# Output projection of a hybrid encoder block in pairs of row blocks: half of its row tiles by seven products of sums instead of eight plain products

## The chip, the cores and the metric

The kernel runs on one core of a Trainium2 chip. The metric is device time in microseconds for one launch; a lower time is better. Before the change the median of three runs is 943.16 us (942.99 to 943.22). One further execution was recorded by the hardware profiler; it took 943.95 us.

The core has a matrix engine (TensorE, called PE in the profile, with its weight loads as PEld), a vector engine (VectorE, DVE), a scalar engine (ScalarE, ACT), a general engine (GpSimd, POOL), and SyncE (SP), which here issues the DMA transfers. Every engine has an instruction stream of its own and waits on semaphores for the others.

## The reference, cut to what matters

One layer: a normalisation, one input projection, windowed attention and a convolution group, both gated, and one output projection with a residual. Only the last lines are touched by the change:

```python
att = windowed_gqa(q, k, v, sink).reshape(B, L, W_ATT) * jax.nn.silu(g_att)
cnv = conformer_conv(c_val, c_glu, conv_w, conv_b, ln_w, ln_b) * jax.nn.silu(g_conv)
mixed = jnp.concatenate([att, cnv], axis=-1)
return z + jnp.einsum('ble,ed->bld', mixed, w_out)
```

`mixed` has 1024 columns: 512 of attention and 512 of the convolution. `w_out` is 1024 x 1024. There are 2304 rows (a prompt of 256 and a sample of 2048), 18 blocks of 128.

## The kernel before, in words

**Numbers in two parts.** Each float32 operand of a large product is split into a high part (`hi`, float32r, a rounding copy on ScalarE) and a low part (`lo`, the rest, a subtraction on VectorE). A product then takes three matmuls: hi x hi, hi x lo, lo x hi (`PASSES`, line 151).

**Two stages.** The first (up to about 605 us) is the input projection in 11 units of weights and two chunks of rows (`ORDER`, line 1068; `items`, line 1070), with the depthwise convolution (31 taps, line 946) on VectorE beside it and the LayerNorm of the convolution's result (`ln_block`, line 211) after it. The second is attention and the output projection, in time slots: `slot_step(s_, slot)` (line 625) has eight slots for each of NB + 2 steps. In step s_ the scores of block s_ are taken (`scores`, one per slot), and in the slots of the next step its probabilities are turned (`bank`, line 491), split and multiplied with v (`pv`, line 522) and merged (`merge`, line 543). Slots are counted through both stages here: slot t is step t // 8, place t % 8. The first 14 slots (`EARLY`) run among the last projection units, through `spread` (line 658); `mixing_open` (line 280), called at the ninth block of the last but one unit, first empties the queue of LayerNorm blocks and then opens the tiles for the mixing, whose places in memory the convolution and LayerNorm held; `attention_rest` (line 679) runs the others.

**The output projection.** The 1024 rows of `w_out` are eight row tiles e of 128; e = 0 to 3 belong to attention and 4 to 7 to the convolution. For block b, column half nh and row tile e, `outproj` (line 601) issues the three matmuls of 512 columns into a PSUM bank of that block and half; the bank gathers all eight e. After the last e, VectorE adds it to the rows of the input (`yo`, loaded by `load_x`), and a DMA stores them. From slot 14 on, every slot takes two such (nh, e) pieces, six matmuls. The last block's second half goes in two quarters of 256 columns, so that the end is short.

**Left operands.** `mix_conv` (line 578) multiplies the convolution's block by its gate on POOL, then splits it into parts: into `mch`, `mcl` for even blocks and into part of `rest` for odd ones. `merge` adds the two halves of the attention's result (VectorE), multiplies by the gate (POOL) and splits into `rest`. `rest` takes the place of the last projection weights and can be written only when the last projection is done.

**The right operand.** `presplit_wo(e)` (line 331) splits the row tiles of `w_out` in the first stage, at places listed in `split_at` (line 1190), and writes the parts to DRAM (`wod`). At the end of the first stage `load_wo` brings all 16 pieces of 512 KB into the tiles that the projection's operands leave (`xh`, `xl`), in the order e = 4 to 7, 0, 1, 2, 3; they stay there.

**What sets the order.** A planner orders the instructions of SP, ACT and DVE (in the first stage also PE's) by the times that it expects; under `manual_schedule` POOL, and from `attention_rest` on PE too, work in the order of the program. Python runs the program's order with a clock of ticks: `tick(ns)` ends each slot or projection group, `later(k, f)` puts f at the k-th tick from now. The taps of the convolution are let out by a credit: a tick gives ns, a tap costs 1.04 x 1167 + 135 ns (line 964), and `owe(ns)` takes credit away, so that other VectorE work puts taps off.

## Time and profile before

| | before |
|---|---|
| median of three runs | 943.16 us |
| the profiled execution | 943.95 us, span 941.9 us |
| PE busy | 935.6 us, 5794 matmuls |
| DVE busy | 744.4 us |
| ACT busy | 421.8 us |
| POOL busy | 293.3 us |
| output projection | 888 matmuls at line 609 |

The span runs from the first to the last instruction of the profiled execution. A row of the page's groups gives line, engine, operation, output<-inputs, shape and count, then busy us and mean ns of one, then the idle time of the engine just ahead of them with what ended it. A row of a timeline gives start, duration, engine, line, operation; "x6" are six merged instructions, and a bracket is idle time before it with its releaser. The matmuls of one group overlap at their ends, so the mean of one is longer than the distance between two; the chain of waits, which counts each stretch of time once, gives the distance.

### The profile page before, as it was taken

The numbers are of one execution on the slowest core, as the hardware profiler recorded it, in microseconds if no ns is written. First come the engines' busy times: TensorE is split into PE (matmuls) and PEld (weight loads), VectorE is DVE, ScalarE is ACT, GpSimd is POOL, SyncE is SP. The second block draws the span as 40 slices with busy tenths as digits, with TensorE's granted clock in tenths as the row PEclk, the third lists the DMA queues.
The fourth block names the chain that finished last, engine by engine and source line by source line (L and its number), as shares of the span: only waits on it lengthen the run. The fifth ranks groups of instructions, "written<-read, shape, count | busy, mean of one in ns | idle before, by whom it ended". The sixth has DMA issues, their size and how long they took to land.

```text
span 941.9 us, 16665 instructions
## 1 busy us (share of the span) xinstructions
PE 935.6 (99%) x5794; PEld 886.3 (94%) x5794; DVE 744.4 (79%) x1263; ACT 421.8 (45%) x1160; POOL 293.3 (31%) x490
## 2 busy tenths in 40 slices
PE   9999999999999999999999999999999999999998
PEld 8999999999999999999999999988888888888887
DVE  5579999997977879999996655677777677767773
ACT  7432022253457751011111356666666666656661
POOL 4320000173558400000000553755433242333332
PEclk9999999999999999999999999999999999999999
DMA  8575345676656595233333697975666556655512
GB/s 306 170 253 217 134 176 176 217 269 251 182 185 189 182 312 182 90 113 134 140 128 123 159 327 225 395 240 159 200 188 172 151 165 196 188 159 148 163 62 68
DMA packets 146211, 176.49 MB, mean 187 GB/s; under 512 B 40816, under 2 KB 108736, under 8 KB 146000
## 3 DMA queue, kind: packets, MB, share of 16 engines
q1 hardware_dynamic: 146128, 175.43, 57.8%
q8 instruction: 46, 0.75, 0.3%
q14 instruction: 37, 0.30, 0.1%
HBM read 112.69 MB, written 62.70 MB: 186 GB/s over the span
## 4 chain that ended last, share of the span: by engine, by line
PE 94%; DMA 2%; DVE 1%; SPq 1%; issue 0%; ACT 0%; POOL 0%; DVEq 0%; ACTq 0%; POOLq 0%
PE pj L863 43%; PE y L609 21%; PE pj L879 13%; PE O L533 5%; PE S L383 4%; PE pT_c L499 2%; PE pT_m L499 2%; PE pT_x L499 1%; DMA cd<-zn 1%; DMA bias<-in_bias_c 1%; PE qT L383 1%; PE lnu L240 0%; DMA xn<-in_z 0%; PE lnt L221 0%; DVE xt L772 0%
## 5 line engine op out<-in xcount | busy, mean ns | idle before, releaser
L863 PE MATMUL pj<-xh,ws 128*128 128x384 f32 (+1 forms) x1536 | 395.9, 338 | 0.1
L946 DVE SCALAR_TENSOR_TENSOR y<-us,cw,y 128x1167 f32<-128x1167 f32 x240 | 329.0, 1427 | 0.4
L863 PEld LDWEIGHTS pj<-xh,ws 128*128 128x128 f32 x1536 | 280.0, 188 | 0.4 <-ACT xh L1111 0.4
L863 PE MATMUL pj<-xl,ws 128*128 128x384 f32 (+1 forms) x768 | 260.9, 340 | 0.1
L609 PE MATMUL y<-wo,rest 128*128 128x512 f32 (+1 forms) x672 | 172.7, 394 | 0.0
L879 PE MATMUL pj<-ws,xh 128*128 128x256 f32 (+1 forms) x880 | 164.2, 284 | 0.3 <-DVE kn L1037 0.3
L863 PEld LDWEIGHTS pj<-xl,ws 128*128 128x128 f32 x768 | 144.1, 188 | 0.5 <-DVE xl L801 0.4
L609 PEld LDWEIGHTS y<-wo,rest 128*128 128x128 f32 x672 | 117.5, 189 | 21.4 <-DVE rest L566 0.3
L879 PEld LDWEIGHTS pj<-ws,xh 128*128 128x128 f32 (+1 forms) x880 | 136.1, 187 | 1.1 <-issue 0.4
L879 PE MATMUL pj<-ws,xl 128*128 128x256 f32 (+1 forms) x440 | 124.3, 283 | 0.0
L441 DVE CUSTOM_DVE_ANT_0 sb<-S,bias,vec 128x304 f32<-128x304 f32 (+5 forms) x144 | 74.5, 517 | 33.8 <-PE S L383 31.5
L453 ACT ACTIVATE sb<-sb,nm 128x304 f32<-128x304 f32 (+5 forms) x144 | 77.8, 540 | 48.9 <-DVE nm L441 48.2
L971 ACT ACTIVATE go<-pj 128x384 f32<-128x384 f32 x48 | 23.5, 489 | 149.8 <-PE pj L863 142.3
L879 PEld LDWEIGHTS pj<-ws,xl 128*128 128x128 f32 (+1 forms) x440 | 82.2, 187 | 0.2
L479 POOL TENSOR_SCALAR sb<-sb,es 128x304 f32<-128x304 f32 (+5 forms) x144 | 73.1, 525 | 16.0 <-DVE es L466 13.1
L561 POOL TENSOR_TENSOR at<-at,ga 128x256 f32<-128x256 f32 x36 | 26.5, 737 | 164.0 <-DVE at L555 104.8
L148 POOL TENSOR_SCALAR ssk<-ssk 128x2 f32<-128x2 f32 x18 | 8.4, 465 | 210.0 <-ACT sqk L985 210.0
L383 PEld LDWEIGHTS S<-kw,q 128*128 128x128 f32 x288 | 53.2, 188 | 10.6
L383 PE MATMUL S<-kw,q 128*128 128x304 f32 (+5 forms) x288 | 62.8, 299 | 0.0
L148 POOL TENSOR_SCALAR ssq<-ssq 128x4 f32<-128x4 f32 (+2 forms) x55 | 23.5, 427 | 98.3 <-ACT xn L726 74.4
L906 ACT ACTIVATE sg<-pj 128x384 f32<-128x384 f32 (+1 forms) x24 | 11.8, 492 | 82.9 <-PE pj L863 82.0
L609 PE MATMUL y<-wo,mch 128*128 128x512 f32 x144 | 47.2, 409 | 0.0
(139 smaller groups left out, 1306.9 us busy)
## 6 DMA issues: line engine op xcount, KB each, us to landing
wd<-ws SPq DMA_DIRECT2D x36, 512.0 KB, 5.8
ws<-wd SPq DMA_DIRECT2D x36, 512.0 KB, 6.2
wraw<-in_w_in SPq DMA_DIRECT2D x52, 256.0 KB, 6.3
xn<-in_z SPq DMA_DIRECT2D x18, 512.0 KB, 5.5
gd<-go SPq DMA_DIRECT2D x48, 192.0 KB, 2.2
yo<-in_z SPq DMA_DIRECT2D x36, 256.0 KB, 3.9
out_y<-yo SPq DMA_DIRECT2D x35, 256.0 KB, 2.7
wo<-wod SPq DMA_DIRECT2D x16, 512.0 KB, 7.4
```

Source lines behind the costliest of these rows:

```text
L148: nc.gpsimd.tensor_scalar(src, src, scale, eps, op0=ALU.mult, op1=ALU.add)
L383: r = f(*a, **k)
L441: nc.vector.tensor_tensor_reduce(out=sb[:, n, c0:c1], in0=ps[:, 0:w], in1=cst["bias"][:, kv, at + c0 : at + c1], scale=1.0, scalar=nsnk[:, ...
L453: nc.scalar.activation(sb[:, n, c0:c1], sb[:, n, c0:c1], AF.Exp, bias=nm[:, n : n + 1], scale=-1.0, accum_out=rs[:, n : n + 1],)
L479: nc.gpsimd.tensor_scalar(sb[:, k, a0:a1], sb[:, k, a0:a1], es[:, k : k + 1], 1.0, op0=ALU.mult, op1=ALU.mult)
L499: nc.tensor.transpose(pt[: c1 - c0, n, :], sbt[b, kv][:, n, c0:c1], ident)
L533: nc.tensor.matmul(opj[b, kv][:, n0:n1], t[:r, kv, :], p[:r, n0:n1], start=(k == "c" and i == 0), stop=(k == "x" and i == len(work) - 1),)
L561: nc.gpsimd.tensor_tensor(at[:, pr, :], at[:, pr, :], gat[b][:, pr, :], op=ALU.mult)
L609: nc.tensor.matmul(ps, mh[mi][:, e % 4, :], wo[e, wi][:, cols], start=(e == 4 and k == 0), stop=(e == 3 and k == 2),)
L863: nc.tensor.matmul(ps[:, :n], ws[:, d, wi, P * half_i : P * half_i + P], x[xi][:, d, o : o + n], start=(k == 0), stop=(k == 3 * ND - 1),)
L879: nc.tensor.matmul(ps[:rows, :UW], x[xi][:, d, o : o + rows], ws[:, d, wi, :], start=(k == 0), stop=(k == 3 * ND - 1),)
L946: nc.vector.scalar_tensor_tensor(y[:, yo + o0 : yo + o1], u[:, o0 + k : o1 + k], cw[:, j, k : k + 1], y[:, yo + o0 : yo + o1], op0=ALU.mul ...
```

## The change

Blocks are taken in pairs p = (b0, b1) = (2p, 2p + 1). Of the eight row tiles four, e = 4, 5 (c, the convolution's) and e = 0, 1 (t, attention's), make a product of two by two blocks: rows b0 and b1, tiles c and t, column halves 0 and 1. Its eight block products become seven products of sums (Strassen's scheme in Winograd's form). Row tiles 6, 7, 2 and 3 stay plain products.

With A = c of b0, B = t of b0, C = c of b1, E = t of b1 on the left, and W11 = c x half 0, W12 = c x half 1, W21 = t x half 0, W22 = t x half 1 on the right, the left operands are c1 = C, s3 = C - A, s2 = A + B - C, s1 = A + B, t0 = B, t1 = E, s4 = E - (A + B - C). The right ones are made once by `presplit_sums` in the first stage on VectorE, split and written to `wod`: there are now 22 pieces of 512 KB in place of 16. All 22 are resident: 18 where the 16 were, two in new tiles `wa0` and `wa1`, two in parts of `pt` and `rest` (`load_apart`). For this `pt` gives up a quarter: the probabilities take turns in three pairs of parts instead of four.

The left sums are taken on POOL: `mix_diff` (C - A), and three sums or differences in `merge`. Each of 11 left operands, two tiles wide, is split by `two_parts` (ACT copy, DVE subtraction of 256 columns) into a place of `rest` (`HOME`); several share a place in turn.

The products of a pair go through two PSUM banks, `BANK`, which change roles with every pair. Products accumulate in a bank over several results, so partial results are taken out on the way: c1 and s2 are copied to SBUF by ACT (`kept`), s3 and s1 are added by DVE from the bank to the row block of y(0,1), and the copies are added on POOL (`add_kept`) to y(1,1), y(0,0) and y(1,0). Thus s3 can start in its bank only when ACT has copied c1 out of it. The four `yo` tiles rotate between the pairs (`yo_at`).

`JOBS` lists the slots: pair p has its products in slots 16p + 15 to 16p + 30, in all 90 matmuls of 512 columns; s3 comes at the end of its slot, after the scores. In the last pair t1 and (1, 0) go in two halves of 256 columns. `acts` lists in which slot loads, gates, splits and additions are issued. Slot 14 has no product. The convolution's half of block 0 has no tile of its own any more; everything that is split waits for `rest`.

```diff
+NS = 2
+PIECES_W = [("c1", 0), ("c1", 1), ("s3", 0), ("s3", 1), ("s2", 0), ("s2", 1), (6, 0), (6, 1), (7, 0), (7, 1)]
+PIECES_W += [("s1", 0), ("s1", 1), ("t0", 0), ("t0", 1), (2, 0), (2, 1), (3, 0), (3, 1)]
+PIECES_W += [("s4", 0), ("s4", 1), ("t1", 0), ("t1", 1)]
+APART = 3
+JOBS = (
+    (15, "c1", (0, 1)),
+    (16, "s3", (0, 1)),
+    (17, "s2", (0, 1)),
+    (18, (0, 0), (6, 7)),
+    (19, "s1", (0, 1)),
+    (20, "t0", (0, 1)),
+    (21, (0, 0), (2, 3)),
+    (22, (1, 1), (6, 7)),
+    (23, (0, 1), (6, 7)),
+    (24, (0, 1), (2, 3)),
+    (25, "s4", (0,)),
+    (26, "s4", (1,)),
+    (26, "t1", (0,)),
+    (27, "t1", (1,)),
+    (27, (1, 0), (6,)),
+    (28, (1, 0), (7,)),
+    (29, (1, 1), (2, 3)),
+    (30, (1, 0), (2, 3)),
+)
+BANK = {"c1": 0, "s3": 0, "t0": 0, "t1": 0, "s2": 1, "s1": 1, "s4": 1, (0, 0): 0, (0, 1): 0, (1, 0): 0, (1, 1): 1}
+OPENS = (("c1", 0), ("s2", 0), ((0, 1), 6), ("t1", 0))
+SUMS = ("c1", "s3", "s2", "s1", "t0", "t1", "s4")
+HOME = {"c1": 0, "t1": 0, "s3": 1, ("c", 0): 1, "s4": 1, "s1": 2, "s2": 3, ("c", 1): 3, "t0": 4, ("t", 0): 5, ("t", 1): 5}
...
+    def presplit_sums(i):
+
+        raw = {}
+        for key, e, nh in ((11, 4 + i, 0), (21, i, 0), (12, 4 + i, 1), (22, i, 1)):
+            raw[key] = sp.tile([P, 2, 400], F32, tag="xt", name=f"wor{key}_{i}", bufs=XTB)[:, :, :UW]
+            src = w_out[e][:, 512 * nh : 512 * nh + 512].rearrange("p (a n) -> p a n", n=UW)
+            nc.sync.dma_start(raw[key], src)
+
+        def operand(name, key):
+            both = sp.tile([P, D], F32R, tag="xn", name=f"wo{name}_{i}")
+            hi, lo = (both[:, 512 * k : 512 * k + 512].rearrange("p (a n) -> p a n", n=UW) for k in range(2))
+            nc.scalar.copy(hi, raw[key])
+            nc.vector.tensor_tensor(lo, raw[key], hi, op=ALU.subtract)
+            owe(700)
+            later(1, lambda: nc.sync.dma_start(wod[PIECES_W.index((name, i))], both.bitcast(F32)))
+
+        def minus(dst, x, y):
+            nc.vector.tensor_tensor(raw[dst], raw[x], raw[y], op=ALU.subtract)
+            owe(700)
+
+        steps = (
+            ("c1", 11, None),
+            ("t1", 21, (11, 12, 11)),
+            ("s4", 22, (12, 22, 12)),
+            ("s1", 11, (22, 22, 11)),
+            ("s3", 12, (21, 21, 22)),
+            ("s2", 22, None),
+            ("t0", 21, None),
+        )
+
+        def step(name, key, diff):
+            operand(name, key)
+            if diff:
+                minus(*diff)
+
+        for k, args in enumerate(steps):
+            later(2 + k, lambda args=args: step(*args))
...
+    def load_apart(i):
+        if i < 2:
+            t = pool["b"].tile([P, D], F32R, tag=f"wa{i}", name=f"wa{i}", bufs=1)
+        else:
+            t = cst["pt" if i < APART else "rest"][:, 6:8].rearrange("p a n -> p (a n)")
+        wo[PIECES_W[i]] = t
+        nc.sync.dma_start(t.bitcast(F32), wod[i])
...
+    def load_x(p, key):
+        r, nh = key
+        rows = NM + P * (2 * p + r)
+        tc.keep_in_program_order(nc.sync.dma_start(yo(p, key), z[rows : rows + P, 512 * nh : 512 * nh + 512]))
...
-            ph, pl = (pt_part(2 * (n_bank[0] % 4) + i) for i in range(2))
+            ph, pl = (pt_part(2 * (n_bank[0] % 3) + i) for i in range(2))
...
+        part = at[:, pr, :]
+        if kv == 0 and r == 0:
+            nc.gpsimd.tensor_tensor(temp(1), part, temp(0), op=ALU.subtract)
+            total = cnt[b][:, 0:NS, :]
+            nc.gpsimd.tensor_tensor(total, total, part, op=ALU.add)
+            work = [("t0", part), ("s2", temp(1)), ("s1", total)]
+        elif kv == 0:
+            nc.gpsimd.tensor_tensor(temp(1), part, temp(1), op=ALU.subtract)
+            work = [("t1", part), ("s4", temp(1))]
+        else:
+            work = [(("t", r), part)]
+
+        for name, x in work:
+            later(2 + (name == "s4"), lambda name=name, x=x: two_parts(name, x))
...
+    def two_parts(name, src):
+        hi, lo = parts(name)
+        nc.scalar.copy(hi, src)
+        nc.vector.tensor_tensor(lo, src, hi, op=ALU.subtract)
...
+    def mix_diff(p):
+        nc.gpsimd.tensor_tensor(temp(0), cnt[2 * p + 1][:, 0:NS, :], cnt[2 * p][:, 0:NS, :], op=ALU.subtract)
+        diff[p] = True
...
-    def outproj(b, nh, e):
-        mh = mix[b, 1 if e < 4 else 0]
-        if e == 4:
-            yps[nh] = psum.tile([P, 512], F32, tag="a" if nh == 3 else "d", name=f"y{b}_{nh}")
-        c0, n = PIECES[nh]
-        ps = yps[nh][:, :n]
-        cols = slice(c0, c0 + n)
-        for k, (mi, wi) in enumerate(PASSES):
-            nc.tensor.matmul(
-                ps,
-                mh[mi][:, e % 4, :],
-                wo[e, wi][:, cols],
-                start=(e == 4 and k == 0),
-                stop=(e == 3 and k == 2),
-            )
-        if e == 3:
-
-            def fin():
-                yo = yot[b, c0 // 512][:, c0 % 512 : c0 % 512 + n]
-                nc.vector.tensor_tensor(yo, ps, yo, op=ALU.add)
-                later(1, lambda: nc.sync.dma_start(out[P * b : P * b + P, cols], yo))
-
-            later(1, fin)
+    def product(p, name, es, c0=0, n=512):
+        if not banks:
+            banks.extend(psum.tile([P, 512], F32, tag="d", name=f"yb{i}") for i in range(2))
+        ps = banks[(BANK[name] + p) % 2]
+        if c0:
+            if "half" not in cst:
+                cst["half"] = psum.tile([P, 512], F32, tag="a", name="yb2")
+            ps = cst["half"]
+        done = es[-1] in (1, 3)
+        for e in es:
+            if name in SUMS:
+                x, i = parts(name), e
+                w = [wo[name, e][:, 512 * k + c0 : 512 * k + c0 + n] for k in range(2)]
+            else:
+                x, i = parts(("c" if e >= 4 else "t", name[0])), e % 4 - NS
+                w = [wo[e, k][:, 512 * name[1] + c0 : 512 * name[1] + c0 + n] for k in range(2)]
+            for k, (mi, wi) in enumerate(PASSES):
+                nc.tensor.matmul(
+                    ps[:, :n],
+                    x[mi][:, i, :],
+                    w[wi],
+                    start=((name, e) in OPENS and k == 0),
+                    stop=(done and e == es[-1] and k == 2),
+                    skip_group_check=True,
+                )
+
+        def add(key, out_too):
+            y = yo(p, key)[:, c0 : c0 + n]
+            nc.vector.tensor_tensor(y, ps[:, :n], y, op=ALU.add)
+            if out_too:
+                r0, q0 = P * (2 * p + key[0]), 512 * key[1] + c0
+                later(1, lambda: nc.sync.dma_start(out[r0 : r0 + P, q0 : q0 + n], y))
+
+        def end():
+            if name in ("c1", "s2"):
+                nc.scalar.copy(kept(name == "s2"), ps)
+            elif name in ("s3", "s1"):
+                add((0, 1), False)
+            elif name in BANK and name not in SUMS and es[-1] == 3:
+                add(name, True)
+
+        if done:
+            later(1, end)
+
+    def add_kept(p, key, i):
+        y = yo(p, key)
+        nc.gpsimd.tensor_tensor(y, y, kept(i), op=ALU.add)
+
+        for rel, f in (
+            (5, lambda b0=b0: load_mix(b0)),
+            (7, lambda b1=b1: load_mix(b1)),
+            (9, lambda p=p: load_x(p, (0, 1))),
+            (10, lambda b0=b0: mix_conv(b0)),
+            (11, lambda b1=b1: mix_conv(b1)),
+            (12, lambda p=p: with_rest(lambda: mix_diff(p))),
+            (12, lambda p=p: load_x(p, (1, 1))),
+            (13, lambda b1=b1: with_rest(lambda: two_parts("c1", cnt[b1][:, 0:NS, :]))),
+            (14, lambda: with_rest(lambda: two_parts("s3", temp(0)))),
+            (17, lambda b0=b0: two_parts(("c", 0), cnt[b0][:, NS:4, :])),
+            (17, lambda p=p: load_x(p, (0, 0))),
+            (20, lambda b1=b1: two_parts(("c", 1), cnt[b1][:, NS:4, :])),
+            (18, lambda p=p: load_x(p, (1, 0))),
+            (18, lambda p=p: add_kept(p, (1, 1), 0)),
+            (20, lambda p=p: add_kept(p, (0, 0), 1)),
+            (21, lambda p=p: add_kept(p, (1, 0), 0)),
+        ):
+            acts.setdefault(16 * p + rel, []).append(f)
+        for rel, name, es in JOBS:
+            to = late_jobs if name == "s3" else jobs
+            if p == LAST and name in ("t1", (1, 0)):
+                for c0 in (0, 256):
+                    to.setdefault(16 * p + rel, []).append((p, name, es, c0, 256))
+            else:
+                to.setdefault(16 * p + rel, []).append((p, name, es))
...
+        t = 8 * s_ + slot
+        with_rest(lambda: None)
+        for f in acts.get(t, ()):
+            f()
...
-        if 8 * s_ + slot >= 16 - AHEAD:
-            for _ in range(2):
-                if todo:
-                    outproj(*todo.pop(0))
+        for job in jobs.get(t, ()):
+            product(*job)
         if has_a:
             scores(a, slot // 4, slot % 4)
...
+        for job in late_jobs.get(t, ()):
+            product(*job)
         tick(2400)
...
+        for k in range(6):
             later(1 + k, lambda k=k: load_wo(12 + k))
-        while slots and (todo or slots[0][0] < NB):
+        later(7, lambda: load_apart(len(PIECES_W) - 1))
+        while slots:
...
+        split_at = {
+            (0, U_C[0], CHUNKS[0][2]): lambda: presplit_wo(6),
+            (0, U_C[1], CHUNKS[0][2]): lambda: presplit_wo(7),
+            (1, U_C[0], CHUNKS[1][0]): lambda: presplit_wo(2),
+            (1, U_C[0], CHUNKS[1][2]): lambda: presplit_wo(3),
+            (1, U_C[1], CHUNKS[1][1]): lambda: presplit_sums(0),
+            (1, U_C[2], CHUNKS[1][2]): lambda: presplit_sums(1),
+        }
```

105 lines of the change are left out of this document (47 added, 58 removed).

## The prediction

> **What bounds the kernel now.** I read the page first, its shares and its chain of waits, then the busy time of pairs of blocks in the steady attention stage. The columns of the second fence are stretch, sum, busy us of PE, PEld, DVE, ACT, POOL, then clock, DMA share and GB/s.
>
> ```profile
> span 941.9 us, 16665 instructions
> PE 935.6 (99%) x5794; PEld 886.3 (94%) x5794; DVE 744.4 (79%) x1263; ACT 421.8 (45%) x1160; POOL 293.3 (31%) x490
> PE 94%; DMA 2%; DVE 1%; SPq 1%; issue 0%; ACT 0%; POOL 0%; DVEq 0%; ACTq 0%; POOLq 0%
> ```
>
> ```profile
> 400.00:500.00 100.00, 100.00 (x569) 100.00 (x568) 100.00 (x77) 12.10 (x23) 0.00 (x0) 1.00 0.35 125
> 580.00:600.00 20.00, 20.00 (x169) 19.83 (x169) 11.58 (x41) 12.28 (x38) 10.63 (x24) 1.00 0.99 342
> 620.00:640.00 20.00, 20.00 (x110) 17.00 (x109) 16.11 (x43) 12.88 (x36) 11.28 (x23) 1.00 0.58 166
> 764.30:802.78 38.48, 38.48 (x217) 33.43 (x217) 28.75 (x75) 24.25 (x63) 13.87 (x22) 1.00 0.60 170
> ```
>
> TensorE is busy 99% of the span, at a granted clock of 1.00 in these stretches, and is 94% of the chain. A pair of blocks takes 38.48 us, all of it PE's; DVE is busy 28.75 (75%), ACT 24.25, POOL 13.87. No other engine sets the pace anywhere after 606 us, so a matmul taken out there is worth its issue time, as long as nothing new makes PE wait.
>
> **What is removed.** The matmuls of the output projection and the place of six of them in the chain of waits (start, us):
>
> ```profile
> L609 PE MATMUL y<-wo,rest 128*128 128x512 f32 (+1 forms) x672 | 172.7, 394 | 0.0
> L609 PE MATMUL y<-wo,mch 128*128 128x512 f32 x144 | 47.2, 409 | 0.0
> L609 PE MATMUL y<-wo,mcl 128*128 128x512 f32 x72 | 28.2, 392 | 0.0
> 687.34 1.40 PE y L609 x6
> 924.77 1.38 PE y L609 x6
> ```
>
> 672 + 144 + 72 = 888, which is 18 blocks x 48, plus 24 because the last block's second half goes in two quarters. The mean of 394 ns counts overlapping matmuls; in the chain six take 1.38 to 1.40 (I use 1.38), so one costs 0.230. Of a pair's 96, half belong to the four chosen row tiles: 8 products of six become 7. That leaves 90, and 9 x 6 = 54 go: 54 x 0.230 = **12.4 us**. The new count should be 810 + 18 = 828.
>
> The Trainium skill (TensorE: Matmul & The Clock Gate, section "Wait — 56ns, not 53.3ns?") puts a warm 512-column matmul at 215.7 ns; by it the estimate is 11.6 us. The chain's 0.230 is this kernel's own figure and I keep it.
>
> **What is added in the steady stage.** The prices per operation (mean ns ahead of the second bar; in the first row least, median, longest):
>
> ```profile
> L566 DVE TENSOR_TENSOR rest<-at,rest x36: 410/554/1033, 611.6 to 933.7; 128x256 fp32r<-128x256 f32 x36
> L587 DVE TENSOR_TENSOR rest<-cn,rest 128x512 fp32r<-128x512 f32 x9 | 6.2, 690 | 0.2
> L620 DVE TENSOR_TENSOR yo<-y,yo 128x512 f32<-128x512 f32 (+1 forms) x37 | 24.8, 670 | 3.7 <-PE y L609 3.7
> L565 ACT CAST rest<-at 128x256 fp32r<-128x256 f32 x36 | 14.6, 406 | 13.8 <-POOL at L561 13.7
> L515 ACT CAST ptiles<-pT_c 128x512 fp32r<-128x512 f32 x36 | 21.1, 587 | 6.8 <-PE pT_c L499 6.0
> L561 POOL TENSOR_TENSOR at<-at,ga 128x256 f32<-128x256 f32 x36 | 26.5, 737 | 164.0 <-DVE at L555 104.8 <-issue 59.2
> L579 POOL TENSOR_TENSOR cn<-cn,gc 128x512 f32<-128x512 f32 x18 | 23.4, 1299 | 0.0
> ```
>
> DVE, per pair: now 2 x 0.69 + 4 x 0.55 + 4 x 0.67 = 6.3; afterwards 11 splits of 256 columns and six additions from PSUM, 11 x 0.55 + 6 x 0.67 = 10.1. That is +3.8, so 32.6 of 38.48 - 1.38 = 37.1 us, 88%. With the shortest split (0.41) it is 31.0, with the longest (1.03) 37.8. ACT: 11 casts of 256 columns and two copies of 512 in place of four and two, so 7 x 0.41 = 2.9 more, 27.1 (73%). POOL: four sums of 256 columns (0.74) and three additions of 512 (1.30), +6.9, so 20.8 (56%). All three fit under PE's 37.1; I cost them at nothing, and what hides them is PE's own queue. If DVE's cover is gone, the price is the last rival below.
>
> POOL works in program order, and behind `add_kept` stand the normalisations that the transposes wait for. `add_kept` of (1,0) at slot 21 waits for a load issued at 18; loads of that kind land in 3.9 us in the middle, and three slots are 3 x 37.1 / 16 = 7.0 us. So nothing there either.
>
> ```profile
> yo<-in_z SPq DMA_DIRECT2D x36, 256.0 KB, 3.9
> ```
>
> **The tight hand-over.** s3 accumulates in the bank that ACT must first copy to `kept`. Between c1 (slot 15) and s3 (late in slot 16) PE has what lies between these products now:
>
> ```profile
> 780.04 0.47 PE L383 MATMUL S<-kw,q 128*128 128x336 f32 x2
> 780.84 0.60 PE L499 MATMUL pT_c<-ident,sb 128*128 128x128 f32 x4
> 781.20 1.63 PE L609 MATMUL y<-wo,rest 128*128 128x512 f32 x6
> 782.66 0.44 PE L383 MATMUL S<-kw,q 128*128 128x304 f32 x2
> 782.94 0.60 PE L499 MATMUL pT_m<-ident,sb 128*128 128x128 f32 x4
> ```
>
> ```profile
> 780.06 0.18 ACT L453 ACTIVATION_READ_ACCUMULATOR sb<-sb,nm 128x1 f32 x1
> 781.09 0.58 ACT L553 COPY tmp<-O 64x512 f32<-64x512 f32 x1 [0.85 <-PE O L533]
> ```
>
> From 780.04 to 781.20 is 1.16, and the next scores add 782.94 - 782.66 = 0.28: 1.44 us of cover. ACT is idle from 780.24 to 781.09, so a 0.59 copy ends near 780.85 and costs nothing. Ordered behind the copy of O it would end at 781.09 + 0.58 + 0.59 = 782.26, against a start of s3 at 781.48: 0.8 us lost per pair. Bounds 0 and 0.8; a gap of this length stands in the row, so I take 0.1, in all **0.9 us**. Other changes of a bank or of a `HOME` place have a product of 1.38 us or more between their two users and are costed at nothing.
>
> **The start of the stage.** Block 0's conv half now has tiles of its own (`mch`), and its products start at once; afterwards slot 14 has no product, and c1, s3 and s2 all need `rest` and POOL:
>
> ```profile
> 606.44 0.61 PE L609 MATMUL y<-wo,mch 128*128 128x512 f32 x2
> 607.80 0.37 PE L383 MATMUL S<-kw,q 128*128 128x208 f32 x2
> 608.36 0.71 PE L609 MATMUL y<-wo,mch 128*128 128x512 f32 x2
> ```
>
> ```profile
> 608.67 0.12 POOL L440 MEMSET sb<- 128x32 f32 x1
> 609.45 1.04 POOL L507 TENSOR_TENSOR ptiles<-ptiles,vec 128x512 fp32r<-128x512 f32 x1
> ```
>
> Slot 14's scores and q transposes take 608.36 - 607.80 = 0.56, so PE would reach c1 at 606.44 + 0.56 = 607.0, and s3 near 609.2 (1.38 of c1, scores 0.2, transposes 0.35, scores 0.2). s3's left operand is made by POOL behind the memset, 608.75 to 609.5; a cast of 0.41 and half a split later it is 610.1: 0.9 late. L507, now at 609.45, gets three more sums of 0.74 in front of it and ends at 609.45 + 2.2 + 1.04 = 612.7, where PE, after s3, wants its O at 611.5: 1.2 more. With 0.2 for the rest, **2.3 us**, once; bounds 0 (another order) and 3.8 (two more sums of 0.74 ahead).
>
> **The early part.** Before, 16 subtractions of 512 columns prepare w_out; afterwards 8 + 24.
>
> ```profile
> L345 DVE TENSOR_TENSOR wor<-wor,wohi 128x512 fp32r<-128x512 f32 x16 | 10.8, 688 | 9.5 <-ACT wohi L344 7.7 <-POOL mv L227 1.7
> 514.75 0.29 DVE L1029 TENSOR_TENSOR vs<-pj,vs 128x128 fp32r<-128x128 f32 x1 [9.07 <-ACT vs L1028]
> 514.96 1.43 DVE L946 SCALAR_TENSOR_TENSOR y<-us,cw,y 128x1167 f32<-128x1167 f32 x1
> 575.22 0.63 PE L240 MATMUL lnu<-ident,zn 128*128 128x128 f32 x4 [0.66 <-DVE zn L234]
> 601.21 1.28 POOL L579 TENSOR_TENSOR cn<-cn,gc 128x512 f32<-128x512 f32 x1
> DMA to landing us min/median/max: 2.8/3.8/9.6
> ```
>
> That is 16 x 0.69 = 11.0 us more on a DVE that is full from 400 to 500, and `owe` puts off 16.1 us of taps (26 x 0.7 against 3 x 0.7). The 9.07 us idle before 514.75 take up most of it if the taps stay ahead; if they fall behind it, among the key and value blocks, 16.1 / 1.35 (a tap's cost in `conv`, 1.04 x 1167 + 135 ns) = 12 taps at 1.43 make the convolution 17 us later, and with it the last LayerNorm transposes, now at 575.22. PE has projections to put in their place. What is late next are the loads into the tiles that LayerNorm frees (the last row is the landing of `cn`), and behind them POOL's product at 601.21. At worst LayerNorm ends at 575.85 + 17 = 592.9, one load takes the longest landing and the next the middle one, 592.9 + 9.6 + 3.8 = 606.3: 5.1 late. Bounds 0 and 5.1; most of the tap delay should go into the idle 9.07, so I take **1.0**. The 3 MB more of w_out pieces (DMA is 0.99 busy from 580 to 600) are needed later than now: the first eight by slot 18 instead of 15.
>
> Tail: after the last O, PE has 18 matmuls of full width, 4.1 us, before ("t",1) is wanted; the chain now takes 934.16 - 930.74 = 3.4:
>
> ```profile
> 930.74 7.95 PE L609 MATMUL y<-wo,rest 128*128 128x256 f32 x54
> 933.74 0.42 DVE L566 TENSOR_TENSOR rest<-at,rest 128x256 fp32r<-128x256 f32 x1 [1.29 <-ACT rest L565]
> ```
>
> **Sum.** The profiled execution took 943.95 (span 941.9 and 2.05 around it), 0.79 above the median. 943.95 - 12.4 + 2.3 + 0.9 + 1.0 = 935.75; less 0.79, **935.0 us**.
>
> **Rivals.** First, ACT's order puts `kept` behind the copy of O in every pair: 9 x 0.8 = 7.2 in place of 0.9, 941.3. For it: ACT has only that one gap; against: the gap precedes the copy of O. Second, LayerNorm comes 17 us later and the loads cost the 5.1: 939.1. For it: taps already stand behind the key and value work; against: 601.21 - 575.85 is 25 us of slack. Third, and slower: DVE cannot be packed as tightly as 88% beside a PE that runs in order. The fullest stretch of the attention stage shown is 16.11 of 20, 80.5%. Were that its limit, a pair would take 32.6 / 0.805 = 40.5, 2.0 more than now, and the whole 943.2 + 18 = 961. It turns slower where DVE's limit lies under 32.6 / 38.48 = 85%. For it: splits vary from 410 to 1033 ns, and the longest fill 37.8 of 37.1 us. Against: DVE's waits in these rows are short, and it is full for 100 us where its work is at hand.
>
> The Trainium skill (SBUF — State Buffer, "SBUF: two separate sides") speaks for this: a GpSimd instruction and a VectorE one with two SBUF inputs take a shared port pair as an exclusive lock, the later one blocked until the other ends. The spread of L566 agrees in sign, and the change adds work on both sides. That the change doesn't do what it says is left out: the count of matmuls is fixed.
>
> **Numbers.** Forecast 0.56 (931.5 to 939); first rival 0.16, half of it under 941.3 and half within 0.2%, about what a measurement here can tell from no change; second 0.12; third 0.16. Faster 0.56 + 0.08 + 0.12 = 0.76, same 0.08, slower 0.16. The low end is the whole 12.4 with no wait, 943.2 - 12.4 = 930.8; the high end takes in the first rival with the start's upper bound, 941.3 + 1.5, and 1.0 more of the early part: 943.8.
>
> **What would show it.** 828 matmuls; a pair near 37.1 us; DVE 31 to 33 us in it; no PE wait on `kept`; a gap of about 2 us between 607 and 613; the last lnu between 576 and 593. A pair at 38.5 or more with PE waiting for DVE would prove me wrong.

## The result, and the profile after

The changed kernel took **955.40 us** (median of 4, 953.70 to 958.93) against 943.16: a ratio of 1.0135 with a 95% interval of 1.0104 to 1.0166, so it is **slower by 1.3%**. The forecast of 935.0 missed by 20 us, and the range (up to 943.8) did not hold it. The profiled execution took 954.25.

The page of the changed kernel, its span, its busy time and the shares of its chain of waits:

```profile
span 952.4 us, 16892 instructions
PE 930.4 (98%) x5734; PEld 878.5 (92%) x5734; DVE 774.5 (81%) x1340; ACT 449.8 (47%) x1233; POOL 364.1 (38%) x553
PE 81%; DVE 6%; POOL 3%; DMA 3%; ACT 3%; issue 2%; SPq 0%; POOLq 0%; ACTq 0%; DVEq 0%
```

TensorE has 60 matmuls fewer (5734 for 5794, so 828 products for 888, the count forecast) and is busy 5.2 us less, yet the span is 10.5 us longer. Its share of the chain fell from 94% to 81%: it now waits for others.

Busy time by stretch, with the columns of the prediction's fence (stretch, sum, PE, PEld, DVE, ACT, POOL, clock, DMA share, GB/s); the last row is one whole pair of blocks:

```profile
580.00:600.00 20.00, 17.60 (x140) 17.33 (x139) 9.15 (x28) 16.52 (x42) 7.07 (x20) 0.91 0.60 205
610.00:620.00 10.00, 5.53 (x26) 4.71 (x27) 4.58 (x10) 4.21 (x12) 3.98 (x7) 0.83 1.07 353
776.68:814.27 37.59, 37.35 (x210) 32.28 (x211) 30.62 (x82) 26.34 (x70) 21.69 (x29) 1.00 0.60 175
```

In the first two rows TensorE stands still for 2.4 and 4.5 us, and its granted clock falls to 0.91 and 0.83; before, it was busy throughout from 580 to 600 at 1.00. A steady pair takes 37.59 in place of 38.48. So the new stage is a little faster, and the way into it much slower.

TensorE's last projection and the first product (timeline):

```profile
616.85 0.58 PE L1030 MATMUL pj<-ws,xh 128*128 128x256 f32 x1 [3.67 <-ACT sqq L1131]
617.23 0.41 PE L1030 MATMUL pj<-ws,xl 128*128 128x256 f32 x1
617.44 0.63 PE L1030 MATMUL pj<-ws,xh 128*128 128x256 f32 x2
617.87 0.41 PE L1030 MATMUL pj<-ws,xl 128*128 128x256 f32 x1
...
619.78 0.28 PE L1030 MATMUL pj<-ws,xl 128*128 128x256 f32 x1
619.90 0.40 PE L1030 MATMUL pj<-ws,xh 128*128 128x256 f32 x2
620.13 0.28 PE L1030 MATMUL pj<-ws,xl 128*128 128x256 f32 x1
...
623.02 0.73 PE L721 MATMUL yb<-wa,rest 128*128 128x512 f32 x2 [1.53 <-ACT rest L679]
```

The first product comes at 623.02, before it was 606.44. From there to the end it is now 952.4 - 623.0 = 329.4 us, before 941.9 - 606.4 = 335.5. **So 16.6 us are lost ahead of the stage and 6 gained in it.** (Some 0.6 of the 16.6 is no loss: a few scores and transposes now stand ahead of the first product, as the prediction has it.) One wait of 3.67 us stands out, for a bank of a projection that ACT frees late.

The chain of waits leads from there back to a store. Below it are SyncE's queue and POOL's product with `cn` in the same stretch (timeline), with the time, the duration and the wait:

```profile
607.26 8.85 DMA qd<-qr
...
616.14 0.37 ACT qr L1155
...
616.85 1.22 PE pj L1030 x4
```

```profile
590.88 3.15 SPq L435 DMA_DIRECT2D wo<-wod  x5
594.13 0.59 SPq L275 DMA_DIRECT2D cd<-zn  x1
594.76 7.02 SPq L435 DMA_DIRECT2D wo<-wod  x7
602.15 1.54 SPq L425 DMA_DIRECT2D wa<-wod  x2
604.66 0.37 SPq L443 DMA_DIRECT2D gc<-gd  x1
605.92 0.33 SPq L445 DMA_DIRECT2D cn<-cd  x1
...
615.83 1.26 POOL L695 TENSOR_TENSOR cn<-cn,gc 128x512 f32<-128x512 f32 x1 [5.43 <-DMA qd<-qr]
```

The last store of LayerNorm (594.13) stands behind five 512 KB pieces of w_out. The loads into the tiles that LayerNorm frees (`wa`, `gc`, `cn`) go out only from 602.15 on: the store took 8.0 us to land among the pieces, 594.13 + 8.0 = 602.13, where two others took 2.0. POOL works in order, so its product with `cn` at 615.83 holds back all that is behind it. (Its row names a query store as the last to come. That one lands at 616.11, after the product has begun; the load of `cn`, sent at 605.92 with a landing of 9.8 us, fits.) A query store sent at 607.26 lands only after 8.85 us, between all these loads. The tile of that query is wanted again by ACT, which is to empty the bank that TensorE waits for. The chain of waits goes through this store and not through POOL's product.

Why LayerNorm is that late is seen in its transposes of the second half of the rows (least, median and longest ns, first and last start). The first fence is the kernel before, the second the changed one; the row of line 946 or 1097 holds the convolution's taps from 498.7 us on:

```profile
L221 PE MATMUL lnt<-ident,y x40: 271/272/273, 531.2 to 568.5; 128*128 128x128 f32 x40
L946 DVE SCALAR_TENSOR_TENSOR y<-us,cw,y x10: 1424/1426/1435, 498.7 to 522.7; 128x1167 f32<-128x1167 f32 x10
```

```profile
L250 PE MATMUL lnt<-ident,y x40: 270/272/273, 543.3 to 582.6; 128*128 128x128 f32 x40
L269 PE MATMUL lnu<-ident,zn x40: 270/272/447, 551.4 to 591.0; 128*128 128x128 f32 x40
L1097 DVE SCALAR_TENSOR_TENSOR y<-us,cw,y x17: 1423/1427/1448, 498.8 to 533.1; 128x1167 f32<-128x1167 f32 x17
```

Seven more taps are left over, the last one is 10.4 us later, and LayerNorm's last transposes, which began at 575.22, are over 15 us later.

### The profile page after: what moved, and what is told of

Same layout as the page of the kernel before. It is cut to its first block, busy times and chain, and to the rows that moved or that the text cites. A ratio compares the mean times of both kernels' runs of the same rounds, so it can differ in the third digit from the quotient of the medians.

```text
span 952.4 us, 16892 instructions
## 1 busy us (share of the span) xinstructions
PE 930.4 (98%) x5734; PEld 878.5 (92%) x5734; DVE 774.5 (81%) x1340; ACT 449.8 (47%) x1233; POOL 364.1 (38%) x553
## 4 chain that ended last, share of the span: by engine, by line
PE 81%; DVE 6%; POOL 3%; DMA 3%; ACT 3%; issue 2%; SPq 0%; POOLq 0%; ACTq 0%; DVEq 0%
PE pj L1014 42%; PE yb L721 16%; PE pj L1030 11%; PE O L616 4%; PE S L466 3%; DVE rest L680 1%; PE pT_m L582 1%; PE pT_c L582 1%; DVE ptiles L599 1%; PE pT_x L582 1%; DVE sb L524 1%; DMA cd<-zn 1%; DMA qd<-qr 1%; ACT sb L536 1%; DMA kd<-ks 1%
## 5 line engine op out<-in xcount | busy, mean ns | idle before, releaser
L721 PE MATMUL yb<-wo,rest 128*128 128x512 f32 (+1 forms) x717 | 190.8, 399 | 0.0
L721 PEld LDWEIGHTS yb<-wo,rest 128*128 128x128 f32 x717 | 125.9, 189 | 22.6 <-DVE rest L680 0.2
L536 ACT ACTIVATE sb<-sb,nm 128x304 f32<-128x304 f32 (+5 forms) x144 | 77.9, 541 | 30.6 <-DVE nm L524 28.5
L177 POOL TENSOR_SCALAR ssk<-ssk 128x2 f32<-128x2 f32 x18 | 10.1, 561 | 211.3 <-ACT sqk L1136 209.3
L562 POOL TENSOR_SCALAR sb<-sb,es 128x304 f32<-128x304 f32 (+5 forms) x144 | 78.3, 563 | 24.7 <-PE pT_x L582 9.9
L732 DVE TENSOR_TENSOR yo<-yb,yo 128x512 f32<-128x512 f32 (+1 forms) x55 | 36.9, 671 | 14.9 <-PE yb L721 14.8
L990 DVE TENSOR_TENSOR ws<-wraw,ws 128x512 fp32r<-128x512 f32 x50 | 34.8, 726 | 8.2 <-ACT ws L989 8.2
```

Source lines behind the costliest of these rows:

```text
L177: nc.gpsimd.tensor_scalar(src, src, scale, eps, op0=ALU.mult, op1=ALU.add)
L536: nc.scalar.activation(sb[:, n, c0:c1], sb[:, n, c0:c1], AF.Exp, bias=nm[:, n : n + 1], scale=-1.0, accum_out=rs[:, n : n + 1],)
L562: nc.gpsimd.tensor_scalar(sb[:, k, a0:a1], sb[:, k, a0:a1], es[:, k : k + 1], 1.0, op0=ALU.mult, op1=ALU.mult)
L721: nc.tensor.matmul(ps[:, :n], x[mi][:, i, :], w[wi], start=((name, e) in OPENS and k == 0), stop=(done and e == es[-1] and k == 2), skip_g ...
L732: nc.vector.tensor_tensor(y, ps[:, :n], y, op=ALU.add)
L990: pinned(eng.tensor_tensor(lo, raw[q], hi, op=ALU.subtract), k < 2)
```

## The experiments

My theory after the result was: the loss is made before the stage, by the preparation of the sums of w_out (`presplit_sums`), through its 15.2 us of work on DVE (22 subtractions of 0.69) and the taps that `owe` puts off for it. One rival was that the new stage itself is slow: its hand-over between banks, its start, and DVE. Another was that the six more pieces of w_out crowd the loads at its start. The kernel before stood at 943.48 us beside the runs named e1 to e4, and at 944.02 beside the others. Times of different groups are compared by how far each lies above its own kernel before.

### The early work, in the kernel before

The kernel before keeps its 16 subtractions and gets 15 more through the same function at the same two places (the second call cut to three steps), with 15 us of put-off (the expectation says 16 of each). That is about what the change adds ahead of the stage: its trace has 30 subtractions in place of 16, and its code puts off 24 x 0.7 = 16.8 us in place of 2.1. What the additional ones store isn't used and isn't loaded.

```diff
+        if i:
+            steps = steps[:2] + (("s4", 22, None),)
...
+            if (c, u, g) == (1, U_C[1], CHUNKS[1][1]):
+                presplit_sums(0)
+            if (c, u, g) == (1, U_C[2], CHUNKS[1][2]):
+                presplit_sums(1)
```

> The kernel before, with 16 additional subtractions (and their casts, loads and stores, to a place in DRAM that nobody reads) and 16 us of credit at the two places where the change puts the sums; the output projection is the old one. Theory A: the last LayerNorm transposes come at 585 to 592 in place of 576, and the old kernel becomes slower by 8 to 16 us, 951 to 959. Rivals B and C: it stays within 2 us of 943.2, because neither the additional loads nor the new products are there.

Measured: 956.87 us, ratio 1.0135 (1.0118 to 1.0152). SyncE's queue and POOL's product look as in the changed kernel:

```profile
590.54 2.84 SPq L403 DMA_DIRECT2D wo<-wod  x5
593.48 0.47 SPq L248 DMA_DIRECT2D cd<-zn  x1
...
613.05 1.26 POOL L622 TENSOR_TENSOR cn<-cn,gc 128x512 f32<-128x512 f32 x1 [3.00 <-DMA cn<-cd]
```

The old stage, with none of Strassen's products and no more pieces to load than before, loses 13.4 us to the preparation alone. The early work explains the whole sign of the result, and both rivals fall as its cause.

The same without the put-off (both `owe` in `presplit_sums` taken out of it):

> The kernel before with the 16 additional subtractions at the same two places but without their 16 us of credit; its output projection is the old one. If the credit is what made LayerNorm late, most of the 13.4 us that the additional work cost the old kernel goes away: 944 to 947, LayerNorm at 578 to 580. If VectorE's work alone does it, it stays at 953 or more.

Measured: 951.09 us, ratio 1.0083 (1.0060 to 1.0106). It lies 7.1 us above its kernel before, between the two times that I had named, and 13.4 with the put-off: the put-off is worth some 6 us in the old kernel. The other 7 belong to the additional work as a whole, the subtractions with their casts, loads and stores, where I had thought that it would nearly hide. That DVE's own time is the price isn't shown. The largest wait that it adds to TensorE is this one:

```profile
563.16 1.09 PE L242 MATMUL lnu<-ident,zn 128*128 128x128 f32 x4 [4.85 <-DVE zn L236]
```

The chain of waits leads from DVE's `zn` back to a LayerNorm store, sent at 557.03, that took 5.05 us to land.

### The put-off alone

The changed kernel, with the work of `presplit_sums` unchanged and its `owe` left out.

```diff
             nc.vector.tensor_tensor(lo, raw[key], hi, op=ALU.subtract)
-            owe(700)
...
             nc.vector.tensor_tensor(raw[dst], raw[x], raw[y], op=ALU.subtract)
-            owe(700)
```

> The changed kernel with the same subtractions in the same place, but without the credit that they take from the convolution's taps (17 us). If under theory A it is the put-off of the taps in the program that makes LayerNorm late, the last LayerNorm transposes come back to about 580 and the time falls to 942 to 945; if it is the 11 us of VectorE work itself, LayerNorm stays at 585 to 591 and the time within 3 us of 955.4. Under rival B or C it stays at 955 in both cases.

Measured: 943.92 us, ratio 1.0004 (0.9995 to 1.0014). That is 0.4 us above its kernel before, where the changed kernel lies 12.2 above its own. **Two lines of bookkeeping make 11.8 us of the loss.** LayerNorm's first transposes and the taps in the views used above:

```profile
L250 PE MATMUL lnt<-ident,y x40: 270/272/274, 531.4 to 572.2; 128*128 128x128 f32 x40
L1095 DVE SCALAR_TENSOR_TENSOR y<-us,cw,y x16: 1423/1428/1434, 499.7 to 533.1; 128x1167 f32<-128x1167 f32 x16
```

The taps end as late as in the changed kernel (the last starts at 533.1 in both), since DVE has the same work. But the first transposes come at 531.4 instead of 543.3. `owe` does not make DVE slower: it moves the taps back in the order in which the program is written. LayerNorm of a block is written down only once the block's last tap is, so it moves back too. TensorE comes to it 12 us later although its input is there: in the changed kernel the last tap ends by 534.6, and no row has TensorE wait at `lnt`.

### SyncE's order alone

The changed kernel with the put-off left in. The stores of LayerNorm and the loads of the pieces keep the order of the program, in which the pieces come last.

```diff
-            later(1, lambda: nc.sync.dma_start(cd[b], st["zn"]))
+            later(1, lambda: tc.keep_in_program_order(nc.sync.dma_start(cd[b], st["zn"])))
...
-        nc.sync.dma_start(t.bitcast(F32), wod[i])
+        tc.keep_in_program_order(nc.sync.dma_start(t.bitcast(F32), wod[i]))
```

> The changed kernel with only the order of SyncE's queue altered: the stores of LayerNorm's results and the loads of the w_out pieces keep their order of the program, so that the last store and the loads of gc and cn for blocks 0 and 1 go out ahead of the twelve pieces. Theory (the store issued at 594.13 behind five pieces lands 8.0 us later, and the loads into the freed tiles wait for it; POOL's product with cn then waits to 615.83): the last store lands 2 to 3 us after its issue near 593, POOL's product comes at 609 to 611, TensorE's wait of 3.7 us near 613 and the low clock there go, last projection matmul at 615 to 618, and 949 to 952. Rival (the loads in front are hidden, the lateness of LayerNorm alone costs the 16 us): last projection matmul at 620 or later, 954 to 957. Second rival (pieces that come later make TensorE wait at the first products): last projection matmul early, but a wait of pieces of several us, 953 to 958.

Measured: 949.70 us, ratio 1.0066 (1.0053 to 1.0080). SyncE's queue and POOL's product:

```profile
593.21 0.32 SPq L275 DMA_DIRECT2D cd<-zn  x1
...
594.55 0.43 SPq L443 DMA_DIRECT2D gc<-gd  x1
...
610.53 1.56 POOL L695 TENSOR_TENSOR cn<-cn,gc 128x512 f32<-128x512 f32 x1
```

The store goes out 0.9 us earlier, `gc` 10.1 us earlier, and POOL's product comes at 610.53, when POOL is through with what stands before it, with no wait. TensorE's wait of 3.67 us is gone. LayerNorm is as late as in the changed kernel (its last transposes are at 591 in both). The kernel lies 5.7 us above its kernel before, not 12.2. So 6.5 us of the loss is the queue, at an unchanged lateness of LayerNorm, and the theory's time (949 to 952) and place (609 to 611) both hold.

The time holds partly by luck. The last projection matmul comes at 611.3, earlier than the 615 to 618 that I expected, and the first product at 615.04. From there to the end it takes 333.3 us, where the changed kernel takes 329.4: the first three distances between copies of c1 are 38.6 to 38.9 us, there 37.1 to 38.3. What the new order costs in these pairs I didn't follow up.

The 6.5 us and the 11.8 of the put-off are not to be added. Without the put-off LayerNorm's last store goes out at 581.20, ahead of the pieces (from 587.53), so their order does no harm. Of the 11.8 us 6.5 go with the order of the queue, and 5.3 stay with the queue in order.

### The preparation in the first half of the rows

The two calls of the changed kernel are moved to chunk 0.

```diff
-            (1, U_C[1], CHUNKS[1][1]): lambda: presplit_sums(0),
-            (1, U_C[2], CHUNKS[1][2]): lambda: presplit_sums(1),
+            (0, U_GC[0], CHUNKS[0][0]): lambda: presplit_sums(0),
+            (0, U_GC[1], CHUNKS[0][1]): lambda: presplit_sums(1),
```

> The changed kernel with the sums of w_out prepared in the first chunk of rows (beside the gate units) instead of beside the second chunk's convolution; nothing else moves. Theory A (the 24 subtractions and the credit they take make the convolution and so LayerNorm 15 us late, and the loads into LayerNorm's tiles come too late): the last LayerNorm transposes return to about 576, the last projection matmul from 621 to about 606, time 955.4 - 15 = 940, with the steady pair unchanged at 37.6. Rival B (the six additional loads of w_out pieces push the loads of the gate and convolution blocks back in the DMA queue): LayerNorm returns to 576, but the last projection stays later than 615, time above 948. Rival C (the loss is made by the new work of the attention stage): little change, above 950.

Measured: 951.25 us, ratio 1.0082 (1.0067 to 1.0098), and not 940. Busy time in chunk 0, first the kernel before, then this one:

```profile
240.00:260.00 20.00, 19.74 (x167) 19.56 (x166) 20.00 (x33) 9.53 (x45) 11.88 (x12) 1.00 0.77 217
```

```profile
240.00:260.00 20.00, 17.84 (x147) 17.22 (x147) 20.00 (x33) 8.63 (x40) 9.29 (x12) 1.00 0.61 155
280.00:300.00 20.00, 16.70 (x139) 16.49 (x138) 17.31 (x22) 13.16 (x67) 15.79 (x21) 0.95 0.53 159
```

DVE had no room here either: it is full from 240 to 260 with and without the sums. TensorE now stands still in these stretches for 2.2 and 3.3 us, and part of the loss has moved here.

With the put-off left out there too (and the new order of the next section):

> The sums of w_out are made in chunk 0, as in the run with the sums there and the new order of products from pair 2 on (948.17), but the put-off of taps (`owe` in `presplit_sums`) is taken out. Theory (the early loss is a delay of work on DVE, of which the put-off is the larger part, wherever it stands): TensorE in chunk 0 loses 3 to 5 us in place of 9.4, the last LayerNorm and the start of the stage come as in the kernel before, shifted by that: last projection matmul at 608 to 611, 941.5 to 944.5. Rival (in chunk 0 the subtractions on DVE cost the delay, since TensorE has no other work there while the taps run; the put-off costs nothing): 947 to 949, no change. Second rival (chunk 0 has room on DVE, so that without the put-off nothing is lost): last projection matmul near 605, 936 to 939.

Measured: 946.30 us, ratio 1.0026 (1.0015 to 1.0037). It lies between the ranges of the theory (up to 944.5) and of the rival (from 947), so it decides for neither; it lies 2.3 us above its kernel before, the same kernel with the put-off (948.17, below) 4.7. These 2.4 us are far from the 11.8 that the put-off costs in chunk 1. In chunk 0 most of the loss remains without it: TensorE waits 5.2 us there for DVE (`kn` and `qs`). Which part of the added work makes DVE late isn't shown.

### The hand-over

On top of the sums in chunk 0, the products of a pair from the second pair on come in the order c1, s2, s3, s1, (0,0). s2 has the other bank, so a whole product lies between c1 and s3.

```diff
+EARLIER = {(17, "s2"): 16, (16, "s3"): 17, (19, "s1"): 18, (18, (0, 0)): 19}
...
-            to = late_jobs if name == "s3" else jobs
+            rel = EARLIER.get((rel, name), rel) if p else rel
+            to = late_jobs if name == "s3" and not p else jobs
```

> As the kernel with the sums in the first chunk, and from the second pair on s2 stands between c1 and s3 (c1, s2, s3, s1, plain product instead of c1, s3, s2, plain product, s1), so that a product of 1.38 us covers the copy of c1 out of its bank. If the wait for that copy (0.24 us in the profile after the modelled end of the transposes) is what separates the pair's 37.58 us from 38.48 - 1.38 = 37.10, the pair falls to 37.1 to 37.2 and the time is 3 to 4 us under that of the kernel with the sums moved alone. If the 0.5 us has another cause, the pair stays at 37.4 to 37.6.

Measured: 948.17 us, ratio 1.0049 (1.0034 to 1.0064), 3.1 us under the kernel with the old order. One of its later pairs, by busy time:

```profile
735.02:772.12 37.10, 37.10 (x212) 32.30 (x211) 30.27 (x82) 26.26 (x70) 22.04 (x29) 1.00 0.62 180
```

The pair takes 37.10 with TensorE never idle, where the changed kernel takes 37.59; eight pairs would give 3.9. Up to the fourth copy of c1 the two orders are equally far apart, and the last five pairs gain 2.8 together. What stands in between in a steady pair is one wait, here in the changed kernel's timeline of ACT and of TensorE:

```profile
775.19 0.55 ACT L536 ACTIVATE sb<-sb,nm 128x304 f32<-128x304 f32 x1 [0.61 <-DVE nm L524]
...
775.86 0.59 ACT L739 COPY keptFalse<-yb 128x512 f32<-128x512 f32 x1
776.47 0.58 ACT L636 COPY tmp<-O 64x512 f32<-64x512 f32 x1
...
776.68 0.52 PE L466 MATMUL S<-kw,q 128*128 128x304 f32 x2 [0.24 <-ACT keptFalse L739]
```

ACT's order has the copy of c1 behind the exponential of the scores, and that waits 0.61 us for DVE. The copy comes ahead of the copy of O, as I had it, but too late by half a microsecond.

### Put-off out and new order: the best of these

> The kernel without the sums' credit, with s2 between c1 and s3 from the second pair on. The two causes shown singly should add: 943.9 without credit, less 8 pairs x (37.58 - 37.10) = 3.8: 940.1, faster than the kernel before by 0.3%. If the order only gains where LayerNorm is late, the pair falls to 37.1 but the total stays above 942.

Measured: 942.75 us against 944.02, ratio 0.9985 (0.9976 to 0.9994), 1.3 us under the kernel before. That is faster than both kernels, before and changed, but by less than the 0.2% from the kernel before that I count as a difference. I expected 3.4 under it, so 2.1 are missing; the other case of my expectation, a total above 942, is what came. Measured each against its own kernel before, the new order brought 1.7 us here, not 3.8. TensorE's waits from 605 to 660 (us in all, times, longest):

```profile
PE O L615 <- POOL ptiles L589: 2.0, 2, 1.6
PE yb L720 <- ACT rest L678: 1.6, 2, 1.0
PE O L615 <- DVE ptiles L598: 0.6, 1, 0.6
PE yb L720 <- DVE rest L679: 0.4, 1, 0.4
PE O L615 <- ACT ptiles L597: 0.4, 1, 0.4
```

They are 5.0 us. In the timeline 2.34 of them stand ahead of the first product or at it (at `O` from 605.18 to 607.08 and at 612.71), 1.62 at 644.05 and 1.05 at 652.56 and 653.73, where the second pair begins. In the kernel before TensorE has no wait in this stretch.

### The sums on POOL

The same kernel, with the subtractions of `presplit_sums` on POOL, which does nothing from 340 to 400 us otherwise.

```diff
-            nc.vector.tensor_tensor(lo, raw[key], hi, op=ALU.subtract)
+            nc.gpsimd.tensor_tensor(lo, raw[key], hi, op=ALU.subtract)
...
-            nc.vector.tensor_tensor(raw[dst], raw[x], raw[y], op=ALU.subtract)
+            nc.gpsimd.tensor_tensor(raw[dst], raw[x], raw[y], op=ALU.subtract)
```

> As the kernel without credit and with the new order, but the 24 subtractions of the sums run on POOL, which does nothing from 350 to 500 us, instead of VectorE. Theory A' (what is left of the lateness is VectorE's own 11 us): the taps of 1.43 us keep their pace, the convolution ends near 524 instead of 534, LayerNorm returns to 575 to 576, and the time falls by 2 to 4 us, to 936 to 938. Rival (a POOL instruction and a VectorE tap with two SBUF inputs shut each other out): each 1.3 us on POOL holds a tap up by as much, 24 x 1.3 = 31 us in place of 11, the convolution ends near 540 or later, and the time rises to 945 or more.

Measured: 945.98 us, ratio 1.0026 (1.0017 to 1.0036), 3.2 us slower than with them on DVE: the rival's time. The groups of DVE and POOL from 340 to 400 us, first with the sums on DVE, then on POOL:

```profile
L1097 DVE SCALAR_TENSOR_TENSOR y<-us,cw,y 128x1167 f32<-128x1167 f32 x32 | 44.8, 1423 | 0.0
```

```profile
L1097 DVE SCALAR_TENSOR_TENSOR y<-us,cw,y 128x1167 f32<-128x1167 f32 x30 | 59.6, 2020 | 0.4
L398 POOL TENSOR_TENSOR wor<-wor,wor 128x512 f32<-128x512 f32 x8 | 18.6, 2321 | 0.5
L1014 PE MATMUL pj<-xh,ws 128*128 128x384 f32 x205 | 54.0, 344 | 4.6 <-DVE us L1069 4.6
```

A tap takes 2020 ns on average beside POOL's subtractions and 1423 without. The 30 taps cost 17.9 us more, which is more than all 22 subtractions took on DVE (22 x 0.69 = 15.2), and TensorE waits 4.6 us for DVE in this stretch.

## Why the prediction was wrong

**The early part failed.** I priced it at 1.0 with an upper bound of 5.1; the first product is 16.6 us late. Three things in that step were wrong:

1. "If they fall behind it": they did. Of the 9.07 us in which DVE idled, 3.8 were filled (the row below, from DVE's timeline), and the taps end 10.4 us later. My worst case for LayerNorm, 592.9, was close to what came: 591.3. The event was seen; it got the wrong chance and the wrong price. The count was off too: the trace has 30 subtractions and not 8 + 24, so 14 x 0.69 = 9.7 us more and not 11.0, and the code puts off 14.7 us more and not 16.1. That error is small and lies on the other side.
```profile
514.98 0.29 DVE L1180 TENSOR_TENSOR vs<-pj,vs 128x128 fp32r<-128x128 f32 x1 [5.32 <-ACT vs L1179]
```

2. I took the put-off for a delay of DVE's work. It is a move in program order, and it takes LayerNorm's place in TensorE's order with it. Leaving it out gives back 11.8 us while the taps end as late.
3. I let the two loads go out as soon as LayerNorm was done, 9.6 + 3.8 us in all. But 6 MB of w_out pieces, needed later but ready, went ahead of them and of the store that frees their tiles: 602.15 + 1.54 to get to `gc`, `cn` at 605.92, POOL's product at 615.83, 14.6 us later than before and not 5.1. TensorE's own wait of 3.67 us came by another way than the one I had priced, through the query store among these loads. Putting only that order right, for both, gives back 6.5.

The step that I used to wave the pieces through ("needed later than now") is what let them do harm: what is needed late and ready early fills a queue.

**The hand-over was mis-sized.** I said 0.1 a pair, bounds 0 and 0.8; it is 37.59 - 37.10 = 0.49 in a steady pair. Where the new order was run it gave back 3.1 and 1.7 us in all, against my 0.9. The first rival (0.8, behind the copy of O) isn't what happened: the copy stands behind an exponential that itself waits. An engine's gap is of use only if its order puts the new work there.

**The start of the stage** was 2.3, bounds 0 and 3.8. In the best kernel the waits up to the first product are 2.34 us. That the size fits is partly luck: I had put the waits at s3 and at the `O` behind it, and they stand at three `O` ahead of the products and at c1. What I left out is the second pair: 1.62 us at 644.05, where POOL takes its product with `cn` for that pair (641.54) ahead of `ptiles` (642.77), and 1.05 for the parts in `rest`. With them it is 5.0, beyond the bound.

**What was right:** the count of 828; the issue time of a matmul, since 38.48 - 37.10 = 1.38 is the six matmuls at 0.230 to the digit, and so 12.4 in all; ACT at 26.34 for 27.1 and POOL at 21.69 for 20.8 in a pair. DVE is at 30.6 for 32.6, just under my shortest case of 31.0. The third rival fell: DVE does 30.27 us of work in 37.10, 82%, and TensorE waits for none of it in a steady pair. (By the 215.7 ns of the Trainium skill's page TensorE: Matmul & The Clock Gate, "Wait — 56ns, not 53.3ns?", the six matmuls would be 1.29 us a pair; the trace decides for 0.230 each.)

**The sum as it came out.** With the put-off gone and the order mended the kernel is at 942.75, 1.3 under its kernel before. Of the 12.4 us saved, then, 11.1 go elsewhere. The profiled executions (943.95, and 941.76 for this kernel, 1.0 under its median) show where. These are TensorE's rows, first of the kernel before, at a place where in both kernels 26 projection matmuls are still to come and the same transposes, scores and `O` lie behind:

```profile
600.77 0.36 PE L383 MATMUL S<-kw,q 128*128 128x176 f32 x2
```

```profile
603.07 0.36 PE L465 MATMUL S<-kw,q 128*128 128x176 f32 x2
```

Up to there the early work costs 2.3 us, and not the 7.1 that it cost the old kernel without the put-off. From there to the end it is 940.0 - 603.07 = 336.9 us in place of 941.9 - 600.77 = 341.1, so 4.2 of the 12.4 arrive and 8.2 don't. The waits above are 5.0 of them; the other 3.2 stand in no row of waits from 605 to 660, and I can't place them. So with the put-off gone most of what is missing lies in the stage and its start, and why the rest of the early work costs 2.3 here and 7.1 in the old kernel stays open.

## What to carry to other kernels

Before pricing new work by how idle its engine is, ask what its bookkeeping moves: a credit that puts work off in program order moves what is written after it, here on TensorE and SyncE too. When something comes late, list what else is ready by then on the same queue: transfers that are needed late and ready early can go first, and the late one then also lands among them (here after 8.0 us in place of 2.0). And price an operation for an idle gap only if that engine's order puts it into the gap.

## What the runs showed of the hardware

**TensorE slows down after the longer waits.** After the 3.67 us wait at 613 in the changed kernel, three 256-column matmuls start in 0.64 us (617.23 to 617.87); from 619.78 to 620.13 it is three in 0.35. The rows of 0.41 go back to 0.28 some 2.7 us after the wait's end. The granted clock from 617.0 to 619.5 is 0.50. The dozen matmuls in between cost about 0.1 us more each, so the wait cost some 1.2 us beyond its length. The Trainium skill (TensorE: Matmul & The Clock Gate, "Part 1: The HAM clock gate (the "warmup" mystery)") has the clock fall to one half after an idle window of about 3.4 us. The trace agrees with the factor (a clock of 0.50; 0.213 us a matmul against 0.117). It differs on the length: the wait of 2.40 us before LayerNorm was followed by transposes at nearly half speed too, four in 1.09 us, where four took 0.63 in the kernel before. In the run with SyncE's order the wait is 2.17 us, and the clock is at 0.51 from 586.9 to 590.2, a microsecond behind the wait's end. A wait of 1.62 us (the kernel with put-off out and new order, at 644.05) left it at 1.00.

```profile
586.01 1.09 PE L269 MATMUL lnu<-ident,zn 128*128 128x128 f32 x4 [2.40 <-DVE mv L254]
```

**A wait here cost twice what its row says.** The hand-over shows 0.24 us of idle TensorE, and the pair lasts 0.49 longer than one without it. As I read it, the ends of matmuls overlap the next start (six take 1.38 us, but are 0.40 each), so a short gap is partly covered by the matmul ahead of it; no run tests this by itself.

**DVE and POOL slow each other down** in the run with the sums on POOL. Taps, which read two operands from SBUF, take 2020 ns on average in place of 1423; the one first tap in this stretch, which reads one, takes 1865 in place of 878. A 512-column POOL subtraction takes 2321 ns where a product of the same form takes 1299 in the attention stage of the kernel before. The Trainium skill (SBUF — State Buffer, "SBUF: two separate sides") says that one holds a shared pair of ports as a lock and the other is blocked until it ends. The sign fits, a tap being 0.6 us longer on average and 0.9 by the median (2348 ns); which of the two holds the lock can't be seen in these rows.
